# Scores of two heads on the two row halves of TensorE in all layers, and a re-ordered even layer, in a two-block transformer on one core

## The chip, the core and the metric

The kernel runs on one core of a Trainium2 chip. The metric is the device time of one execution in microseconds. Before the change it is 2098.92 us, the median of three runs (2097.51 to 2102.35). Three engines matter for this change: TensorE (PE), which does the matmuls and the transposes and whose clock has two levels, 1.2 and 2.4 GHz; VectorE (DVE); and GpSimd (POOL). ScalarE (ACT) does the exponentials, the casts and the copies out of PSUM, and the SP queue issues the loads. Each engine works through its own list of instructions in order and waits on semaphores for the others.

## The reference, cut to what matters

The input has 256 tokens of width 1024. A first block of two layers is followed by a second block of an even and an odd layer. Every layer of the first block has a hybrid mixer of three attentions, then an attention to a memory and a feed-forward (in layer 0 a SwiGLU, in layer 1 a mixture of eight experts). The even layer has a 16-head causal attention and, beside it, a state space model.

```python
# hybrid mixer, per layer: 4 heads of 64 (neighborhood), 8 query heads on 2 key heads of 64 (GQA), 4 heads of 96 (MLA)
ya = neighborhood_attention(a_q, a_k, a_v, na_rpb)
yb = blocked_attention(qb.reshape(b, s, GQA_KV_HEADS, GQA_GROUP, HEAD_DIM), kb, vb, HEAD_DIM ** -0.5)
yc = blocked_attention(q_full, k_full, vc, (MLA_NOPE + MLA_ROPE) ** -0.5)
merged = gates[0] * (ya @ w_proj_a) + gates[1] * (yb @ w_proj_b) + gates[2] * (yc @ w_proj_c)

# even layer: rotation of the first 16 of 64 columns of each head, causal attention, and the state scan
rot = jnp.concatenate([x1 * cos - x2 * sin, x2 * cos + x1 * sin], axis=-1)
scores = jnp.einsum('bhqd,bhqkd->bhqk', q_blk, k_g)
_, states = lax.associative_scan(combine, (a_seq, bu), axis=1)      # 32 groups of 64 complex states
y = gelu(real(states @ c) + d_skip * u); y = y * sigmoid(y @ glu_w + glu_b)
```

## The kernel before, in words

**Linear layers.** A weight arrives in f32 by DMA, ACT casts it to a high part (L201) and DVE or POOL subtracts that from it for a low part (L203, `..._l`). Each product is three matmuls (L219 to L221). In the even layer every low part is made on POOL, as 128x1024 subtractions. The names say the weight: `weu` (state input), `weq` (queries and keys), `wev` (values), `wega` and `wegs` (gates of the attention and of the state branch), `wglu` (the linear layer behind the state branch, which needs all of its outputs), `wg` and `wp` (gates and projections of the hybrid mixer).

**Attention in the hybrid mixer.** `attend` walks over pairs of heads. For each head `att_scores` (matmul at L412) makes a 256 x 256 score in one bank of PSUM, two matmuls of 64 rows (96 for MLA). DVE takes the row maximum, ACT the exponential, PE transposes (L446), and `att_pv` multiplies by the values. The 64-row operands lie on partitions 0 to 63 or 64 to 127: in a neighborhood pair one head on each half, in a GQA pair (heads 2b and 2b+1, which share a key head) both on the same.

**Even layer.** `even` runs about from 1668 to 1877 us of the trace. `state` makes the state input. `qk(i, c)` makes queries or keys of eight heads (i says which, c which half) and rotates them by six DVE products (L1400) before four transposes per half of the tokens (L1404). `attend(b)` handles two heads: scores (L1335, L1336), maximum (L1341 on DVE), exponential (L1345, ACT), reciprocal (L1346, DVE), scaling (L1348, ACT), transposes (L1356), a copy (L1357, ACT) and the product with the values (L1366, L1367). The state model is a generator `ssm` with 16 steps, here called pairs: two groups of states each. A pair has two matmuls into one bank (`bu`, L1273, 32 rows), then fifteen DVE instructions in that bank (L1282 to L1304: rotation, two scans in two halves, rotation back). After each four pairs come sixteen matmuls (`sy`, L1311), a DVE sum (L1314) and the GELU.

**PSUM.** There are three banks `ps`, two `sc`, one `pv` and two `tp` (the transposes'). In the even layer `bu` alternates between a `ps` and an `sc` bank, the scores are in `sc`, and the transposes in `tp`.

**What sets the order.** A scheduler in the framework takes the program's order of emission as the priority, and puts each engine's instructions in the order in which its own model says that they become ready. The program emits `state`, `qk(0,0)`, `qk(1,0)`, two pairs, `values(0)`, one pair, and then eight `attend(b)` with two pairs behind each but the first, with the remaining `qk`, `values` and `gate_s` between them.

Of the kernel before, what the change touches and what calls it, by code (L numbers as in the profile page):

```python
# [19 lines left out]
P = 128  # L20
T = 256
# [75 lines left out]
class Net:  # L97
# [305 lines left out]
        return xo  # L403


    def att_scores(self, q, k):

        ps = self.mmps("sc", "sc")
        n = len(q)
        for t in range(2):  # L410
            for j in range(n):
                self.nc.tensor.matmul(ps[:, ts(t, T)], q[j][:, ts(t, P)], k[j], start=(j == 0), stop=(j == n - 1))  # L412
        return ps

    def att_probs(self, ps, scale, bias=None, pr=None):
# [40 lines left out]
    def att_pv(self, vs, pTs):  # L456

        ps = self.mmps("pv", "pv")
        for i in range(2):
            o = ps[64 * i:64 * i + 64, :T]  # L460
            for kb in range(2):
                self.nc.tensor.matmul(o, vs[i][kb], pTs[i][:, kb], start=kb == 0, stop=kb == 1, skip_group_check=True)
        return ps[:, :T]

    def rope(self, dst, src, cos, sin, half, tmp):
# [22 lines left out]
    def hybrid(self, x, l):  # L488
# [73 lines left out]
        def attend(pairs, y0, scale, bias=None):  # L562

            def finish(b, hs, pTs):
                o = self.att_pv([vv for _, _, vv in hs], pTs)
                self.split(o, yT[0][:, y0 + b], yT[1][:, y0 + b])
            for b, hs in enumerate(pairs):
                pTs = []
                for i, (q, k, _) in enumerate(hs):
                    pr = None  # L570
                    if bias is not None:
                        pr = act.tile([P, 2, T], F32, tag="pr", name="nab", bufs=4)
                        nc.sync.dma_start(pr, bias[2 * b + i].rearrange("(t q) k -> q t k", q=P))
                    pTs.append(self.att_pT(self.att_probs(self.att_scores([q], [k]), scale, pr, pr)))
                finish(b, hs, pTs)

        def hv(f, h):
# [36 lines left out]
        ml = [[(qcT[:, 2 * b + i], kcT[:, 2 * b + i], [vc[t][:, 2 * b + i] for t in range(2)]) for i in range(2)]  # L614
              for b in range(2)]
        attend(ml, 6, 96 ** -0.5)
        attend([[gq(2 * b), gq(2 * b + 1)] for b in range(4)], 2, 0.125)


        gt, mg, mx = {}, [], []  # L620
# [638 lines left out]
    def ssm(self, u):  # L1259
# [6 lines left out]
        for po in range(4):  # L1266
            del zs[:]
            for pq in range(4):
                p = 4 * po + pq
                rows = slice(32 * pq, 32 * pq + 32)  # L1270
                ps = self.mmps("bu", ("ps", "sc")[p % 2])
                for j in range(2):
                    mm(ps[:, ts(j, T)], self.bmat[rows, po, j], u[rows, po], start=True, stop=True,  # L1273
                       tile_position=(32 * pq, 0))
                c = self.rot[:, 0, p, :HT].unsqueeze(1).to_broadcast(B)
                s = self.rot[:, 1, p, :HT].unsqueeze(1).to_broadcast(B)
                m1 = act.tile([P, 2, T], F32, tag="sm1", name="sm1", bufs=5)
                q = [act.tile([P, 2, T], F32, tag="sm2", name="sm2", bufs=4) for _ in range(2)]
                z = ps.rearrange("p (j t) -> p j t", t=T)
                zr = ps.rearrange("p (j t) -> p j t", t=HT)  # L1280
                qr = [a.rearrange("p j t -> p (j t)").rearrange("p (j t) -> p j t", t=HT) for a in q]
                v.tensor_tensor(qr[0], zr, s, op=ALU.mult)  # L1282
                v.tensor_tensor(zr, zr, c, op=ALU.mult)
                v.tensor_tensor(z[:, 0], z[:, 0], q[0][:, 1], op=ALU.add)
                v.tensor_tensor(z[:, 1], z[:, 1], q[0][:, 0], op=ALU.subtract)
                r = self.decay[:, p:p + 1].to_broadcast([P, HT])
                init = [0.0, 0.0]
                for h in range(NH):
                    if h:
                        ini = self.sm.tile([P, 2], F32, tag="sini", name="sini")  # L1290
                        e = h * HT - 1
                        v.tensor_scalar(ini, z[:, :, e], self.rot[:, 0, p, HT:HT + 1], None, op0=ALU.mult)
                        v.scalar_tensor_tensor(ini[:, 0:1], z[:, 1, e:e + 1], self.nsin[:, p:p + 1], ini[:, 0:1],
                                               op0=ALU.mult, op1=ALU.add)
                        v.scalar_tensor_tensor(ini[:, 1:2], z[:, 0, e:e + 1], self.rot[:, 1, p, HT:HT + 1],
                                               ini[:, 1:2], op0=ALU.mult, op1=ALU.add)
                        init = [ini[:, 0:1], ini[:, 1:2]]
                    for j in range(2):
                        o = z[:, j, ts(h, HT)]
                        v.tensor_tensor_scan(o, r, o, init[j], op0=ALU.mult, op1=ALU.add)  # L1300
                v.tensor_tensor(qr[1], zr, s, op=ALU.mult)
                v.tensor_tensor(zr, zr, c, op=ALU.mult)
                v.tensor_tensor(m1[:, 0], z[:, 0], q[1][:, 1], op=ALU.subtract)
                v.tensor_tensor(m1[:, 1], z[:, 1], q[1][:, 0], op=ALU.add)  # L1304
                zs.append(m1)
                if pq < 3:
                    yield
# [20 lines left out]
        self.nc.scalar.activation(s, u, AF.Tanh, scale=0.5)  # L1328
        self.nc.vector.scalar_tensor_tensor(dst, s, 1.0, u, op0=ALU.add, op1=ALU.mult)

    def causal_probs(self, pr, q, k, scale, bias):

        nc, v = self.nc, self.nc.vector
        ps = self.mmps("sc", "sc")
        nc.tensor.matmul(ps[:, :P], q[:, :P], k[:, :P], start=True, stop=True)  # L1335
        nc.tensor.matmul(ps[:, P:3 * P], q[:, P:], k, start=True, stop=True)  # L1336
        mx, ng, sm = (self.sm.tile([P, 2], F32, tag=n, name=n, bufs=4) for n in ("mx", "ng", "sm"))
        cols = [slice(0, P), slice(P, 3 * P)]
        parts = [pr[:, c] for c in cols]
# [20 lines left out]
    def causal_pv(self, vs, pTs):  # L1360

        ps = self.mmps("pv", "pv")
        mm = self.nc.tensor.matmul
        for i in range(2):
            o = ps[64 * i:64 * i + 64, :T]
            mm(o, vs[i][0], pTs[i][:, :T], start=True, stop=False, skip_group_check=True)  # L1366
            mm(o[:, P:], vs[i][1], pTs[i][:, T:], start=False, stop=True, skip_group_check=True)  # L1367
        return ps[:, :T]

    def even(self, x):  # L1370
# [18 lines left out]
        def qk(i, c):  # L1389
# [7 lines left out]
            lo, hi = h4[:, :, :, :8], h4[:, :, :, 8:16]  # L1397
            for o, p, q, op in ((t1, lo, si, ALU.mult), (t2, hi, si, ALU.mult), (lo, lo, co, ALU.mult),
                                (hi, hi, co, ALU.mult), (lo, lo, t2, ALU.subtract), (hi, hi, t1, ALU.add)):
                v.tensor_tensor(o, p, q, op=op)  # L1400
            for t in range(2):
                tp = self.tps()
                for b in range(4):
# [10 lines left out]
        def attend(b):  # L1414
            if b % 2:
                prs = [self.sm.tile([P, 512], F32, tag="lnf", name="epr", bufs=LNF) for i in range(2)]
            else:
                prs = [self.keep.tile([P, 512], F32, tag=n, name="epr") for n in ("lngt", "lnbt")]
            pTs = [self.causal_pT(self.causal_probs(prs[i][:, :3 * P], *(a[64 * i:64 * i + 64, b] for a in qkT),
                                                    0.125, bias)) for i in range(2)]  # L1420
            if b % 2 == 0:
                self.lin_feat(x, w, 3072 + P * b, 256, lambda i, ps: gate(b + i, ps), name="wega")
            o = self.causal_pv([[vv[:, t, 64 * (2 * b + i):64 * (2 * b + i) + 64] for t in range(2)]
# [6 lines left out]
        with self.phase("ssm"):  # L1430
# [11 lines left out]
                              name="wegs")  # L1442
            state()
            self.hold = None
            qk(0, 0)
            qk(1, 0)
            step(2)
            values(0)
            step(1)
            late = [lambda: qk(0, 1), lambda: qk(1, 1), lambda: values(1), lambda: gate_s(0), lambda: gate_s(1)]  # L1450
# [112 lines left out]
def layout(inputs):  # L1563
# [8 lines left out]
    order = np.arange(a["w_in"].shape[2])  # L1572
    order[768:1280] = 768 + np.arange(512).reshape(2, 4, 64).transpose(1, 0, 2).reshape(-1)
    I["w_in"] = a["w_in"][:, :, order]

    def cols(v):
        return v.reshape(-1, P).T
# [77 lines left out]
```

## Time and profile before

The profiled execution took 2097.21 us by the clock of the runs, and its trace has a span of 2095.4 us. The median of the three runs is 1.7 us above the profiled execution.

| what | value |
|---|---|
| runs, us | 2102.35, 2097.51, 2098.92 |
| profiled execution, us | 2097.21 |
| its span in the trace, us | 2095.4 |
| PE busy, share of the span | 96% |
| DVE busy | 79% |
| ACT busy | 62% |
| POOL busy | 13% |

PE is busy nearly everywhere, so a microsecond of PE work is in most places a microsecond of time. The exception is where PE's busy share falls. Rows of the timeline give the start of a group of like instructions, its length, the engine, the line, the operation with output and inputs, and the count; a bracket at the end holds the idle time before it and the instruction that ended it. The trace shows two instructions for each f32 matmul of the program, so a score of two matmuls has four rows in it.

### The profile page before, as it was taken

The page shows a single profiled execution, that of the slowest core. Times are in us where ns is not written, and L with a number is a line of the kernel's source. Part 1 is how long each engine was busy: PE and PEld are TensorE (multiplying, and loading weights), DVE is VectorE, ACT ScalarE, POOL GpSimd, SP SyncE. Part 2 cuts the span into 40 slices and gives each one's busy share as a digit, 9 for nine tenths or more (in the row PEclk, how much of TensorE's full clock was granted, in tenths as well). Part 3 has the DMA queues.
Part 4 walks back from the last instruction along what each step waited for, and adds up shares of the span by engine and source line. Part 5 has one row for each costly group of instructions (what it writes and reads, how often), then busy time and mean ns, then how long its engine had stood idle before and what let it go on. Part 6 is the DMA issues. An engine that isn't in the chain of part 4 may idle for free. (4 is left out here: it accounts for less than half of the span.)

```text
span 2095.4 us, 31534 instructions
## 1 busy us (share of the span) xinstructions
PE 2008.7 (96%) x11112; PEld 1706.1 (81%) x11112; DVE 1647.7 (79%) x2958; ACT 1302.9 (62%) x1968; POOL 280.4 (13%) x169
## 2 busy tenths in 40 slices
PE   8999998999999999899999999999999799968998
PEld 8877898998987888688888888888888587737996
DVE  7775765555786676799999999999999747987984
ACT  5665545444666454777887787778778545624452
POOL 2000223000400140200000000000000375402400
PEclk9999999999999999899999999999999799969999
DMA  8544545555644548699999899999999664305562
GB/s 284 165 137 148 188 147 166 185 182 188 209 142 131 191 154 288 225 338 359 345 343 350 290 366 312 367 317 372 311 394 327 209 178 122 108 27 158 182 197 95
DMA packets 300423, 481.84 MB, mean 230 GB/s; under 512 B 18528, under 2 KB 117856, under 8 KB 300256
## 3 DMA queue, kind: packets, MB, share of 16 engines
q1 hardware_dynamic: 300256, 479.75, 68.0%
q8 instruction: 89, 1.46, 0.3%
q14 instruction: 78, 0.64, 0.1%
HBM read 478.63 MB, written 1.05 MB: 229 GB/s over the span
## 5 line engine op out<-in xcount | busy, mean ns | idle before, releaser
L203 DVE TENSOR_TENSOR we_l<-we_r,we_h 128x1024 fp32r<-128x1024 f32 (+1 forms) x188 | 208.2, 1129 | 12.0 <-ACT we_h L201 8.9
L201 ACT CAST we_h<-we_r 128x1024 fp32r<-128x1024 f32 (+1 forms) x188 | 181.4, 978 | 53.9 <-PE eg L220 22.1
L221 PE MATMUL ea<-we_l,xgh 128*128 128x512 f32 (+1 forms) x384 | 146.6, 382 | 0.4 <-DVE we_l L203 0.4
L219 PE MATMUL ea<-we_h,xgh 128*128 128x512 f32 (+1 forms) x384 | 144.9, 377 | 0.9 <-ACT xgh L210 0.9
L219 PE MATMUL eg<-we_h,xgh 128*128 128x512 f32 (+1 forms) x384 | 145.6, 379 | 0.0
L221 PE MATMUL eg<-we_l,xgh 128*128 128x512 f32 (+1 forms) x384 | 144.8, 377 | 0.4 <-DVE we_l L203 0.2
L220 PE MATMUL ea<-we_h,xgl 128*128 128x512 f32 (+1 forms) x384 | 144.8, 377 | 0.3 <-DVE xgl L211 0.3
L220 PE MATMUL eg<-we_h,xgl 128*128 128x512 f32 (+1 forms) x384 | 143.7, 374 | 0.0
L203 DVE TENSOR_TENSOR we_l<-more,we_h 128x1024 fp32r<-128x1024 f32 (+1 forms) x120 | 133.5, 1132 | 12.7 <-ACT we_h L201 10.0
L221 PE MATMUL ey<-wd_l,ehh 128*128 128x512 f32 x352 | 138.2, 396 | 1.8 <-DVE wd_l L203 1.6
L201 ACT CAST we_h<-more 128x1024 fp32r<-128x1024 f32 (+1 forms) x120 | 116.0, 978 | 38.1 <-PE eg L220 13.3
L220 PE MATMUL ey<-wd_h,ehl 128*128 128x512 f32 x352 | 138.1, 392 | 0.0
L219 PE MATMUL ey<-wd_h,ehh 128*128 128x512 f32 x352 | 138.0, 392 | 0.0
L203 POOL TENSOR_TENSOR weu_l<-we_r,weu_h 128x1024 fp32r<-128x1024 f32 x4 | 9.4, 2372 | 793.1 <-ACT weu_h L201 793.1
L203 DVE TENSOR_TENSOR wd_l<-wd_r,wd_h 128x1024 fp32r<-128x1024 f32 x87 | 103.8, 1217 | 1.8 <-ACT wd_h L201 1.1
L219 PE MATMUL gu<-xh,wgu_h 128*128 128x256 f32 x352 | 100.9, 287 | 0.9 <-ACT xh L210 0.9
L201 ACT CAST wd_h<-wd_r 128x1024 fp32r<-128x1024 f32 x87 | 90.0, 1052 | 17.9 <-PE ey L220 16.5
L220 PE MATMUL gu<-xh,wgu_l 128*128 128x256 f32 x352 | 100.6, 286 | 0.0
L221 PE MATMUL gu<-xl,wgu_h 128*128 128x256 f32 x352 | 100.3, 286 | 0.0
L201 ACT CAST wres_h<-wres_r 128x1024 fp32r<-128x1024 f32 x54 | 56.6, 1052 | 68.1 <-PE ps L220 59.4
L203 DVE TENSOR_TENSOR wgu_l<-wgu_r,wgu_h 128x1024 fp32r<-128x1024 f32 x44 | 55.4, 1259 | 51.0 <-ACT wgu_h L201 51.0
L203 DVE TENSOR_TENSOR wres_l<-wres_r,wres_h 128x1024 fp32r<-128x1024 f32 x46 | 56.1, 1224 | 43.1 <-ACT wres_h L201 42.6
(631 smaller groups left out, 6513.5 us busy)
## 6 DMA issues: line engine op xcount, KB each, us to landing
we_r<-in_moe_w_gu_dram SPq DMA_DIRECT2D x156, 512.0 KB, 5.4
more<-in_moe_w_gu_dram SPq DMA_DIRECT2D x100, 512.0 KB, 5.6
wd_r<-in_moe_w_down_dram SPq DMA_DIRECT2D x87, 512.0 KB, 7.4
more<-in_moe_w_down_dram SPq DMA_DIRECT2D x60, 512.0 KB, 7.2
rt<-in_moe_w_gu_dram SPq DMA_DIRECT2D x49, 512.0 KB, 5.5
wg_r<-in_w_in_dram SPq DMA_DIRECT2D x48, 512.0 KB, 3.7
wgu_r<-in_ffn_w_gu_dram SPq DMA_DIRECT2D x44, 512.0 KB, 4.5
rt<-in_moe_w_down_dram SPq DMA_DIRECT2D x29, 512.0 KB, 7.5
```

Source lines behind the costliest of these rows:

```text
L201: nc.scalar.copy(H[:, a:b], r)
L203: sub.tensor_tensor(L[:, a:b], r, H[:, a:b].bitcast(F32), op=ALU.subtract)
L219: mm(ps, sH, mH, start=first, stop=False, skip_group_check=skip)
L220: mm(ps, sL, mH, start=False, stop=False, skip_group_check=skip)
L221: mm(ps, sH, mL, start=False, stop=last, skip_group_check=skip)
```

## The change

There are two parts, and the number of matmuls stays as it was.

**Hybrid mixer.** `att_scores` now takes a list of heads and walks over the two halves of the queries in the outer loop, over the heads in the inner one, with one `sc` bank for each head. Pairs of 64-row heads go in together; MLA heads go in one by one, as before. The GQA pairs are now heads b and b+4, which lie on different row halves, and the rows of `w_proj_b` are permuted on the host to match. In `att_pv` the loop over the key blocks is the outer one.

**Even layer.** All `bu` banks are `sc` banks. The scores of both heads are made together by `causal_scores`, in the `tp` banks. The six products of each rotation are issued on GpSimd, 24 in all. `causal_pv` interleaves its two heads. The order of emission has two pairs ahead of `qk(0,0)` and one each behind `qk(0,0)`, `qk(1,0)` and `values(0)`: five pairs instead of three ahead of the first `attend`.

```diff
-    def att_scores(self, q, k):
-        ps = self.mmps("sc", "sc")
-        n = len(q)
-        for t in range(2):
-            for j in range(n):
-                self.nc.tensor.matmul(ps[:, ts(t, T)], q[j][:, ts(t, P)], k[j], start=(j == 0), stop=(j == n - 1))
+    def att_scores(self, heads):
+        ps = [self.mmps("sc", "sc") for _ in heads]
+        for t in range(2):
+            for o, (q, k) in zip(ps, heads):
+                self.nc.tensor.matmul(o[:, ts(t, T)], q[:, ts(t, P)], k, start=True, stop=True)
...
+                split = all(q.shape[0] == 64 for q, _, _ in hs)
+                if split:
+                    sc = self.att_scores([(q, k) for q, k, _ in hs])
...
-        attend([[gq(2 * b), gq(2 * b + 1)] for b in range(4)], 2, 0.125)
+        attend([[gq(b), gq(b + 4)] for b in range(4)], 2, 0.125)
...
-                ps = self.mmps("bu", ("ps", "sc")[p % 2])
+                ps = self.mmps("bu", "sc")
...
+    def causal_scores(self, heads):
+        ps = [self.tps("sc") for _ in heads]
+        for cols, keys, qs in ((slice(0, P), slice(0, P), slice(0, P)), (slice(P, 3 * P), slice(0, T), slice(P, T))):
+            for o, (q, k) in zip(ps, heads):
+                self.nc.tensor.matmul(o[:, cols], q[:, qs], k[:, keys], start=True, stop=True)
+        return ps
...
-                v.tensor_tensor(o, p, q, op=op)
+                nc.gpsimd.tensor_tensor(o, p, q, op=op)
...
+            step(2)
             qk(0, 0)
+            step(1)
             qk(1, 0)
-            step(2)
+            step(1)
             values(0)
             step(1)
```

On PE, at the start of the even layer's queries, the first two pairs stand here before: `bu` is the output of a pair's matmuls, `su` the state input and `ssb` the state matrix.

```order
11747 L219 MATMUL ps<-weq_h,xh 128x512
11748 L220 MATMUL ps<-weq_h,xl 128x512
11749 L1273 MATMUL bu<-su,ssb 128x256
11750 L221 MATMUL ps<-weq_l,xh 128x512
11751 L219 MATMUL ps<-weq_h,xh 128x512
```

And on PE in the changed kernel, where the first two pairs stand right behind the last `weu` matmul and the first two `weq` matmuls:

```order
11658 L221 MATMUL ps<-xl,weu_h 128x256
11659 L219 MATMUL ps<-weq_h,xh 128x512
11660 L220 MATMUL ps<-weq_h,xl 128x512
11661 L1276 MATMUL bu<-su,ssb 128x256 x4
11662 L221 MATMUL ps<-weq_l,xh 128x512
```

Two pairs moved from the middle of the `weq` matmuls, one pair's first matmul at a time, to their very start.

On PE, at the end of the even layer, the rows ahead of the first `wglu` matmul before: `tp` are the transposes of the probabilities, `pv` the product with the values, `sy` the outputs of four pairs.

```order
12387 L1273 MATMUL bu<-su,ssb 128x256 x2
12388 L1356 MATMUL tp<-ident,epr 128x128 x3
12389 L1366 MATMUL pv<-pT,ev 64x256
12390 L1367 MATMUL pv<-pT,ev 64x128
12391 L1356 MATMUL tp<-ident,epr 128x128 x3
12392 L1366 MATMUL pv<-pT,ev 64x256
12393 L1367 MATMUL pv<-pT,ev 64x128
12394 L1311 MATMUL sy<-sm_26501,ssck 32x256
```

And on PE in the changed kernel, the last pair and what follows it:

```order
12337 L1276 MATMUL bu<-su,ssb 128x256 x2
12338 L1374 MATMUL pv<-pT,ev 64x256
12339 L1364 MATMUL tp<-ident,epr 128x128
12340 L1339 MATMUL sc<-ekT,eqT 128x128
12341 L1339 MATMUL sc<-ekT,eqT 128x256
12342 L1364 MATMUL tp<-ident,epr 128x128 x2
12343 L1374 MATMUL pv<-pT,ev 64x256
12344 L1376 MATMUL pv<-pT,ev 64x128 x2
12345 L1339 MATMUL sc<-ekT,eqT 128x128
12346 L1339 MATMUL sc<-ekT,eqT 128x256
12347 L1314 MATMUL sy<-sm_26381,ssck 32x256
```

The last pair now stands ahead of the last two heads' scores, and the scores of two heads (`sc`) stand apart, with transposes of the earlier head between them; so it is for the head pairs 3 to 7, while 0 to 2 stand together.

On POOL, between the low parts of the queries' and the values' weights, this stands in the changed kernel (before, the second row is followed at once by the sixth):

```order
71 L203 TENSOR_TENSOR weq_l<-we_r,weq_h 128x1024 x2
72 L203 TENSOR_TENSOR weq_l<-weq_r,weq_h 128x1024 x6
73 L1409 TENSOR_TENSOR etmp<-rt,rope_e 128x128 x2
74 L1409 TENSOR_TENSOR rt<-rt,rope_e 128x16x8 x2
75 L1409 TENSOR_TENSOR rt<-rt,etmp 128x16x8 x2
76 L203 TENSOR_TENSOR wev_l<-wev_r,wev_h 128x1024 x4
```

The six products of a rotation came onto POOL's queue as a block between the weights' low parts.

## Rows read from the trace of the kernel before

**Rows 1.** Windows: stretch, length, busy us per engine (instructions), PE clock, DMA share, GB/s.
```profile
100.00:200.00 100.00, 100.00 (x492) 77.95 (x492) 67.71 (x133) 56.59 (x107) 0.00 (x0) 1.00 0.45 138
600.00:700.00 100.00, 100.00 (x496) 77.92 (x496) 70.83 (x150) 57.41 (x115) 0.00 (x0) 1.00 0.46 135
1830.00:1840.00 10.00, 5.05 (x32) 3.36 (x34) 9.67 (x22) 2.70 (x5) 0.00 (x0) 0.76 0.52 158
1840.00:1872.00 32.00, 17.18 (x60) 7.69 (x60) 28.87 (x82) 7.14 (x22) 0.00 (x0) 0.50 0.00 1
```
**Rows 2.** Waits of PE, 1668 to 1880 us: line, waited for, total, times, longest.
```profile
PE sy L1311 <- DVE sm L1303: 14.8, 3, 5.4
PE bu L1273 <- DVE mx L1341: 3.3, 1, 3.3
```
**Rows 3.** Timeline of PE: scores of the hybrid mixer, line L412.
```profile
62.84 1.14 PE L412 MATMUL sc<-naqk 64*128 64x256 f32 x8
65.63 1.13 PE L412 MATMUL sc<-naqk 64*128 64x256 f32 x4
67.23 0.70 PE L412 MATMUL sc<-naqk 64*128 64x256 f32 x2
68.23 0.70 PE L412 MATMUL sc<-naqk 64*128 64x256 f32 x2
136.04 1.99 PE L412 MATMUL sc<-kb,qb 64*128 64x256 f32 x8
665.75 1.99 PE L412 MATMUL sc<-kb,qb 64*128 64x256 f32 x8
```
**Rows 4.** Timeline of DVE in the even layer: a rotation, and pairs.
```profile
1696.04 2.19 DVE L1400 TENSOR_TENSOR etmp<-rt,rope_e 128x128 f32<-128x128 f32 x2 [11.63 <-ACT rt L1387]
1709.07 0.69 DVE L1282 TENSOR_TENSOR sm<-bu,rot 128x512 f32<-128x512 f32 x1 [10.04 <-PE bu L1273]
1723.49 0.68 DVE L1282 TENSOR_TENSOR sm<-bu,rot 128x512 f32<-128x512 f32 x1
1746.91 0.69 DVE L1282 TENSOR_TENSOR sm<-bu,rot 128x512 f32<-128x512 f32 x1 [1.63 <-PE bu L1273]
1863.04 0.68 DVE L1282 TENSOR_TENSOR sm<-bu,rot 128x512 f32<-128x512 f32 x1
1870.11 0.41 DVE L1304 TENSOR_TENSOR sm<-bu,sm 128x256 f32<-128x256 f32 x1
```
**Rows 5.** Windows as in rows 1: the even layer in two stretches.
```profile
1731.00:1745.00 14.00, 14.00 (x65) 9.81 (x64) 6.43 (x26) 10.92 (x28) 7.14 (x4) 1.00 0.31 92
1745.00:1872.00 127.00, 106.50 (x618) 76.89 (x616) 116.54 (x329) 59.01 (x140) 40.35 (x17) 0.85 0.30 94
```
**Rows 6.** Line L1400, 1740 to 1790 us: operation, count, ns min/median/max, first and last start.
```profile
L1400 DVE TENSOR_TENSOR etmp<-rt,rope_e x4: 279/595/1891, 1748.1 to 1764.8; 128x128 f32<-128x128 f32 x4
L1400 DVE TENSOR_TENSOR rt<-rt,rope_e x4: 277/279/280, 1750.7 to 1766.5; 128x128 f32<-128x128 f32 x4
L1400 DVE TENSOR_TENSOR rt<-rt,etmp x4: 273/276/282, 1751.8 to 1767.2; 128x128 f32<-128x128 f32 x4
```
**Rows 7.** Timeline of POOL in the even layer.
```profile
1695.50 2.38 POOL L203 TENSOR_TENSOR weq_l<-weq_r,weq_h 128x1024 fp32r<-128x1024 f32 x1 [0.32 <-ACT weq_h L201]
1701.72 9.62 POOL L203 TENSOR_TENSOR wev_l<-wev_r,wev_h 128x1024 fp32r<-128x1024 f32 x4 [3.85 <-ACT wev_h L201]
```
**Rows 8.** Timeline of PE: a score of head pair 3, a head's scores, the end.
```profile
1796.51 0.49 PE L1335 MATMUL sc<-ekT,eqT 64*128 64x128 f32 x2
...
1841.78 0.79 PE L1335 MATMUL sc<-ekT,eqT 64*128 64x128 f32 x2
1842.37 1.06 PE L1336 MATMUL sc<-ekT,eqT 64*128 64x256 f32 x2
...
1872.09 0.58 PE L219 MATMUL ps<-sgxh,wglu_h 128*128 128x256 f32 x1
```
**Rows 9.** Timeline of ACT: the copy that ends that head's chain.
```profile
1852.72 0.48 ACT L1357 COPY pT<-tp 128x384 f32<-128x384 f32 x1 [0.50 <-PE tp L1356]
```

More of the change, by code (lines that the diff above doesn't have):

```diff
@@ L458, in att_pv @@
         ps = self.mmps("pv", "pv")
[L459 to L462, printed above, removed]
+        for kb in range(2):
+            for i in range(2):
+                self.nc.tensor.matmul(ps[64 * i:64 * i + 64, :T], vs[i][kb], pTs[i][:, kb], start=kb == 0,
+                                      stop=kb == 1, skip_group_check=True)
         return ps[:, :T]
@@ L573, in attend @@
                         nc.sync.dma_start(pr, bias[2 * b + i].rearrange("(t q) k -> q t k", q=P))
-                    pTs.append(self.att_pT(self.att_probs(self.att_scores([q], [k]), scale, pr, pr)))
+                    pTs.append(self.att_pT(self.att_probs(s, scale, pr, pr)))
                 finish(b, hs, pTs)
@@ L1329, in silu2, with causal_probs @@
         self.nc.vector.scalar_tensor_tensor(dst, s, 1.0, u, op0=ALU.add, op1=ALU.mult)
-    def causal_probs(self, pr, q, k, scale, bias):
+    def causal_scores(self, heads):
[4 more added lines that the diff above has]
+        return ps
+    def causal_probs(self, pr, ps, scale, bias):
         nc, v = self.nc, self.nc.vector
-        ps = self.mmps("sc", "sc")
-        nc.tensor.matmul(ps[:, :P], q[:, :P], k[:, :P], start=True, stop=True)
-        nc.tensor.matmul(ps[:, P:3 * P], q[:, P:], k, start=True, stop=True)
         mx, ng, sm = (self.sm.tile([P, 2], F32, tag=n, name=n, bufs=4) for n in ("mx", "ng", "sm"))
@@ L1363, in causal_pv @@
         mm = self.nc.tensor.matmul
+        o = [ps[64 * i:64 * i + 64, :T] for i in range(2)]
         for i in range(2):
-            o = ps[64 * i:64 * i + 64, :T]
-            mm(o, vs[i][0], pTs[i][:, :T], start=True, stop=False, skip_group_check=True)
-            mm(o[:, P:], vs[i][1], pTs[i][:, T:], start=False, stop=True, skip_group_check=True)
+            mm(o[i], vs[i][0], pTs[i][:, :T], start=True, stop=False, skip_group_check=True)
+        for i in range(2):
+            mm(o[i][:, P:], vs[i][1], pTs[i][:, T:], start=False, stop=True, skip_group_check=True)
         return ps[:, :T]
@@ L1418, in attend @@
                 prs = [self.keep.tile([P, 512], F32, tag=n, name="epr") for n in ("lngt", "lnbt")]
-            pTs = [self.causal_pT(self.causal_probs(prs[i][:, :3 * P], *(a[64 * i:64 * i + 64, b] for a in qkT),
-                                                    0.125, bias)) for i in range(2)]
+            sc = self.causal_scores([[a[64 * i:64 * i + 64, b] for a in qkT] for i in range(2)])
+            pTs = [self.causal_pT(self.causal_probs(prs[i][:, :3 * P], sc[i], 0.125, bias)) for i in range(2)]
             if b % 2 == 0:
@@ L1574, in layout @@
     I["w_in"] = a["w_in"][:, :, order]
+    I["w_proj_b"] = a["w_proj_b"][:, order[768:1280] - 768]
     def cols(v):
```

1 line of the change is left out of this document (added).

## Prediction

> **What bounds the kernel now.** I first read the windows, because the share of busy time over the whole span hides the stages. In the two stretches of the hybrid mixer that hold its GQA scores, PE is busy for all of the 100 us, at the full clock, while DVE has a third of its time left [rows 1]. There the kernel is bound by PE, and a microsecond taken from PE is a microsecond of time. In the even layer this turns over. From 1830 us PE is busy for 5.05 of 10 us, then for 17.18 of 32 us at a granted clock of 0.50, the level of 1.2 GHz, and DVE is busy for 38.5 of the 42 us [rows 1]. There the end is set by DVE. The view of waits says what is late: PE's `sy` matmuls wait 14.8 us in all for the last DVE instructions of a pair, and one `bu` waits 3.3 us for a score bank that DVE empties [rows 2]. What counts as the end of the even layer is the first `wglu` matmul, at 1872.09 [rows 8], since it needs all of the pairs. So I cost the hybrid part by PE time and the even part by DVE's work ahead of that matmul.
>
> **Scores in the hybrid mixer.** Two heads on different row halves, four matmuls, lasted 1.14 us (a neighborhood pair at 62.84). Two on the same half, with as many columns, lasted 1.99 (GQA, the first at 136.04, the last of eight at 665.75) [rows 3]. So the row halves work at the same time, and the GQA pairs should go from 1.99 to 1.14: 8 x 0.85 = 6.8 us. The second neighborhood pair of a layer was torn into three pieces, 1.13 + 0.70 + 0.70 = 2.53 us [rows 3]; its four matmuls now come together, 1.39 us less. The rows of the timeline overlap by nearly 0.1 us with what follows each piece, so I take 1.2, and twice for the two layers: 2.4 us. The MLA scores stay. Sum: 9.2 us, all of it on the path, since PE has no gap there [rows 1]. The low end is below nothing: a pair now takes both `sc` banks at once, so the next pair's scores wait for DVE's maxima of both heads. DVE has 32 us of every 100 free [rows 1], which speaks against such a wait, but if each of the 12 pairs of row-half heads in both layers lost 0.8 us, the gain would be gone, and at 1.5 us it would be a loss of 9. I take 9.2, since PE has other matmuls to do between the pairs. The interleaving in `att_pv` changes no count and its heads were already side by side: nothing.
>
> **Pairs moved forward in the even layer.** DVE waited 11.63 us for the first rotation and 10.04 us for the first pair, which began at 1709.07; the third began at 1723.49, and the fourth only at 1746.91, when its matmul had come; between 1731 and 1745 DVE was busy for 6.43 of 14 us [rows 4, 5]. The changed order on PE has two pairs at the start of `weq` and three more before the first `attend`, then two again where the fourth and the fifth stood. So at 1745 DVE will have five pairs behind it rather than three, and the two moved ones went into time in which it was idle. A pair costs DVE 7.48 us from the start of the last L1282 to the end of its L1304 [rows 4], less two instructions of 0.33 us of the pair before that lie in between: 6.8. Two pairs are 13.6 us.
>
> **Rotations on GpSimd.** Of the four rotations the last two lie behind 1745. Their twelve products took 279 ns each at the least, but the first of each lasted up to 1891 ns [rows 6], some 5 us together. The first rotation shows why: its first product started at 1696.04 and, with the next, took 2.19 us, while POOL's subtraction ran from 1695.50 to 1697.88 [rows 4, 7]. The two earlier rotations lie where DVE was idle and bring nothing. The Trainium skill, SBUF — State Buffer, "SBUF: two separate sides", says that VectorE and GpSimd share one pair of ports under an exclusive lock, so that a VectorE instruction with two SBUF inputs and a GpSimd instruction never run at once; the trace agrees, by the 2.19 us just named. By that rule the moved products still stop DVE's instructions of that kind. The twelve products would then give 12 x 0.30 = 3.6 of the 5 us back, as an estimate by that page's lock, and the forecast would be 3.6 us later.
>
> On POOL the price has no row. The bounds are DVE's 0.28 us for the same product [rows 6] and POOL's 2.38 us for eight times the columns [rows 7]; by columns 2.38 / 8 = 0.30, and I take that, since L203 is the same operation with two inputs. Six products are 1.8 us. They stand in POOL's queue ahead of the low parts of `wev`, which would wait behind them; POOL had 3.85 us idle there, waiting for ACT [rows 7], so they fit. That cover is gone from 0.64 us per product on. At 2.38 us a block of six would hold POOL for 14.3 us and PE would wait 10 us for `wev`; I keep this end for the range.
>
> **Banks.** `bu` in `sc` banks alone removes the tie of a `bu` bank to a weight's `ps` bank and to the scores' maxima; 3.3 us of PE's waits were of that kind [rows 2], inside the stretch that DVE sets, so they are worth nothing by themselves. Three head pairs have their scores together on the two row halves. One head's scores took 1.65 us at the half clock (1841.78 to 1842.37 + 1.06) [rows 8], 0.83 at the full one, so PE gets 3 x 0.83 = 2.5 us back, but PE doesn't set the end. The `tp` banks are where a new wait can come from (rival 3).
>
> **The sum.** From 1745 to 1872 DVE was busy for 116.5 us and idle for 10.5 [rows 5]. Without two pairs and two rotations 97.9 us are left. With the same idle time the `wglu` matmul starts at 1745 + 97.9 + 10.5 = 1853.4. DVE is now less far behind PE and will wait for it more often, between 0 and 6 us more; I take 2.6, so 1856, 16 us earlier. The end that PE alone would set is 1830 + 5.05 + 17.18 / 2 = 1843.6 at the full clock [rows 1], less 2.5 for the scores: 1841. DVE stays later than that, so 1856 stands. What follows `wglu` moves along as a whole. 2097.2 - 9.2 - 16 = 2072.0 for an execution like the profiled one; the median of the runs is 1.7 above it, so 2073.7.
>
> **Rivals.**
> 1. *PE becomes the bound.* If DVE keeps up, `wglu` starts at 1841, 31 us earlier: 2097.2 - 9.2 - 31 + 1.7 = 2058.7. For it: DVE's remaining 97.9 us fit into the 96 us from 1745 to 1841 almost exactly. Against it: that needs a DVE that never waits, and it waited 10.5 us before.
> 2. *The even layer gains nothing.* If the maxima, exponentials and transposes of the last heads form the path rather than DVE's sum of work, the end stays at 1872 and only the hybrid part is left: 2097.2 - 9.2 + 1.7 = 2089.7. For it: in the changed order scores, transposes and value products of the last heads alternate on PE up to the end.
> 3. *The `tp` banks make the heads go one after the other; slower.* In the head pairs 3 to 7 a head's scores now take one of the two banks through which the transposes go, and the second head's scores stand behind the first one's transposes. One head's chain, from its score at 1841.78 to the end of its copy at 1853.20, is 11.4 us [rows 8, 9]. Head pair 3 began at 1796.51 [rows 8]. Ten chains with nothing overlapped end at 1796.5 + 114 = 1910.5, 38.4 us later than before, and the time is 2097.2 - 9.2 + 38.4 + 1.7 = 2128. It is slower than before by more than the measurement tells from ten chains of 8.9 us on (1872.1 + 9.2 + 4.2 = 1885.5). Against it: much of the 11.4 us is DVE at other pairs' work, which is lighter now, and one head needs its bank only until its maximum is taken.
> 4. *The row halves bring nothing* (the change doesn't do what it says): the even part alone, 2097.2 - 16 + 1.7 = 2082.9. Against it stands 1.14 next to 1.99 us [rows 3].
>
> **How the numbers follow.** The forecast, with the even part between 10 and 22 us, gets 0.52. Rival 1 gets 0.13, rival 2 gets 0.17, rival 3 gets 0.07, rival 4 gets 0.04. For a loss in the even layer that cancels the hybrid gain (between rivals 2 and 3) I leave 0.07. A measurement of this kernel tells some 0.2%, 4.2 us, from no change. Faster is then 0.52 + 0.13 + 0.17 + 0.04 = 0.86, the same 0.07, slower 0.07. The range goes up to 2090, which takes in rival 2, and down to 2062, which leaves out half of rival 1 and so holds about 0.8.
>
> **What would show it.** The GQA scores should be groups of eight rows of 1.14 us. DVE's first L1282 (now L1285) should start near 1686, five of them should lie ahead of the first maximum's end, and the first `wglu` should come some 25 us earlier in the span, of which some 9 are there when the even layer starts. POOL's products should last about 0.3 us. PE should still wait for DVE ahead of the last `sy`, at half clock, but for less time. The prediction is wrong if PE waits in the hybrid mixer for maxima, if DVE shows idle time of more than 17 us between 1745 and the end, or if PE waits for weights' low parts behind POOL's products.

## The result, and the profile after

The changed kernel takes 2075.63 us, the median of four runs (2073.2 to 2080.89), against 2098.64 for the kernel before in the same comparison (2097.51 to 2102.35). The ratio is 0.9891, with a 95% interval of 0.9867 to 0.9914. The forecast was 2073.7 us, within 2062 to 2090. The span in the trace went from 2095.4 to 2072.5 us.

Where the 23 us went can be read off PE's timeline, since the order of the matmuls is nearly the same in both kernels. I compare the start of the same matmul in both, at the borders of the stages:

| border | before | after | gained so far |
|---|---|---|---|
| first `wc` (hybrid mixer, layer 0) | 40.91 | 40.41 | 0.50 |
| first `wres` behind it | 211.11 | 206.12 | 4.99 |
| first `wc`, layer 1 | 548.35 | 543.42 | 4.93 |
| first `wres` behind it | 719.42 | 710.32 | 9.10 |
| first expert matmul | 851.10 | 840.50 | 10.60 |
| first `weq` (even layer) | 1683.44 | 1672.45 | 10.99 |
| first `wglu` | 1872.09 | 1849.09 | 23.00 |
| end of the span | 2095.4 | 2072.5 | 22.9 |

The two hybrid mixers give 4.49 and 4.17 us, 8.7 together. The memory attention of layer 1 gives another 1.5 us; its code is the same, and the granted clock between 700 and 800 us was 0.98 before and 1.00 after. The even layer, from the first `weq` to the first `wglu`, went from 188.65 to 176.64 us: 12.0. I call these 176.64 us "the stretch" from here on.

The scores of the hybrid mixer, timeline of PE after (start, length, engine, line, operation, output and input, rows and columns, form, count):

```profile
62.34 1.13 PE L411 MATMUL sc<-naqk 64*128 64x256 f32 x8
65.65 1.55 PE L411 MATMUL sc<-naqk 64*128 64x256 f32 x8
134.34 1.13 PE L411 MATMUL sc<-kb,qb 64*128 64x256 f32 x8
...
657.91 1.14 PE L411 MATMUL sc<-kb,qb 64*128 64x256 f32 x8
```

The GQA pairs went from 1.99 [rows 3] to 1.13 or 1.14 us, all eight. The second neighborhood pair came together, but took 1.55 us; the run with the loops swapped shows why.

The even layer, windows of the kernel after (stretch, length, busy us and instructions of PE, PE's loads, DVE, ACT and POOL, then PE's clock, the DMA share and GB/s):

```profile
1720.00:1734.00 14.00, 14.00 (x70) 10.84 (x69) 4.43 (x12) 11.40 (x24) 11.57 (x6) 1.00 0.49 143
1734.00:1849.00 115.00, 103.48 (x592) 75.68 (x590) 99.13 (x294) 60.29 (x148) 42.93 (x28) 0.87 0.30 98
1802.00:1814.00 12.00, 8.72 (x30) 6.30 (x31) 11.38 (x35) 5.73 (x18) 2.36 (x1) 0.57 0.13 45
```

The first two answer to [rows 5], shifted by the 11 us gained ahead of them. DVE's work in the second fell from 116.5 to 99.1 us, and its idle time rose from 10.5 to 15.9. The third shows a stretch at a granted clock of 0.57, most of it at the level of 1.2 GHz, in the middle of the layer; the kernel before does not have it there.

The timeline of DVE after, with its idle times in brackets:

```profile
1674.17 0.69 DVE L1285 TENSOR_TENSOR sm<-bu,rot 128x512 f32<-128x512 f32 x1 [0.77 <-PE bu L1276]
...
1698.94 0.69 DVE L1285 TENSOR_TENSOR sm<-bu,rot 128x512 f32<-128x512 f32 x1 [4.34 <-PE bu L1276]
1712.57 0.48 DVE L1317 SCALAR_TENSOR_TENSOR su<-su,pp,sy 128x256 f32<-128x256 f32 x1 [6.67 <-PE sy L1314]
1714.01 0.69 DVE L1285 TENSOR_TENSOR sm<-bu,rot 128x512 f32<-128x512 f32 x1 [0.96 <-PE bu L1276]
1734.20 0.42 DVE L1435 TENSOR_TENSOR sil<-pv,ega 128x256 f32<-128x256 f32 x1 [7.54 <-PE pv L1376]
1735.25 0.69 DVE L1285 TENSOR_TENSOR sm<-bu,rot 128x512 f32<-128x512 f32 x1 [0.63 <-PE bu L1276]
```

The first pair starts at 1674.17 instead of 1709.07 [rows 4], the fifth at 1714.01, and the sixth at 1735.25. DVE still waits 6.67 and 7.54 us between them.

What PE waits for in the even layer after, 1657 to 1860 us (line, waited for, total, times, longest):

```profile
PE tp L1364 <- ACT epr L1356: 9.4, 4, 4.5
PE pv L1374 <- ACT pT L1365: 2.1, 3, 1.0
```

The wait of `sy` for DVE, 14.8 us before [rows 2], is gone from this view. PE now waits 9.4 us with its transposes for scaled probabilities, and the wait of `bu` for score maxima is gone as well.

### The profile page after: what moved, and what is told of

Read it like the earlier page. It is cut to its first block, busy times and chain, and to the rows that moved or that the text cites. A ratio compares the mean times of both kernels' runs of the same rounds, so it can differ in the third digit from the quotient of the medians.

```text
span 2072.5 us, 31525 instructions
## 1 busy us (share of the span) xinstructions
PE 1992.7 (96%) x11112; PEld 1694.1 (82%) x11112; DVE 1634.5 (79%) x2934; ACT 1301.8 (63%) x1968; POOL 290.9 (14%) x193
```

## The experiments

Each kernel below is given with its time, and with the first `weq` and the stretch in the trace of one of its executions. The times of one kernel differ by 0.6 to 7.7 us from execution to execution. The places in a trace are exact to some hundredths, but they hold for that one execution. The kernel before took 2100.89, 2099.33 and 2097.56 us (medians) beside the three groups of runs.

| kernel | time, us | first `weq` | stretch | span |
|---|---|---|---|---|
| before | 2098.64 | 1683.44 | 188.65 | 2095.4 |
| after | 2075.63 | 1672.45 | 176.64 | 2072.5 |
| hybrid mixer alone | 2089.09 | 1672.01 | 191.74 | 2086.8 |
| even layer alone | 2085.05 | 1683.62 | 175.08 | 2083.2 |
| pairs' order of before | 2083.32 | 1672.28 | 185.22 | 2081.0 |
| banks of before | 2072.59 | 1673.48 | 176.08 | 2072.8 |
| rotations on DVE | 2074.94 | 1672.60 | 176.41 | 2073.1 |
| no rotations | 2074.03 | 1671.95 | 175.94 | 2072.1 |
| GQA on the same row half | 2081.59 | 1680.33 | 175.08 | 2079.8 |
| heads one after the other | 2081.46 | 1677.48 | 181.31 | 2081.7 |
| after, once more | 2074.16 | 1672.82 | 176.64 | 2072.9 |
| two more pairs ahead | 2071.02 | 1672.66 | 165.21 | 2069.3 |
| one more pair ahead | 2069.29 | 1672.19 | 169.13 | 2067.3 |
| two more pairs, banks of before | 2067.59 | 1673.87 | 167.46 | 2066.3 |

### Each half of the change alone

The edit is the diff's own: the hybrid part put into the kernel before, and the even part put into the kernel before.

> The kernel before with the change of the hybrid mixer alone (scores of two heads on the row halves, GQA pairs b and b+4); the even layer as before. Theory (row halves work at the same time, PE sets the end there): the first weq matmul of the even layer starts 9 to 11 us earlier than the 1683.44 of before, as in the changed kernel (1672.45), and the stretch from the first weq to the first wglu matmul stays at 188.7 +- 1 us; the time is 2088 +- 2. Rival (the two parts act only together, by freeing banks or the queue): less than 5 us earlier at weq, or a stretch that is shorter than 186.

Measured: 2089.09 us (2088.32 to 2090.19), the ratio to the kernel before 0.9945 (0.9928 to 0.9961). The first `weq` came 11.4 us earlier, a little more than expected. The stretch was not the same: 191.74, 3.1 us longer with the same code as before. PE's rows are equal to 0.02 us for the first 127 us of it, and then part:

```profile
1799.00:1807.00 8.00, 8.00 (x34) 5.73 (x33) 6.53 (x25) 4.00 (x14) 0.28 (x1) 0.57 0.19 66
```

This is a window of the hybrid part alone. PE was busy for all of its 8 us, but at a granted clock of 0.57. In the kernel before the same matmuls, 11 us later, ran at 1.00:

```profile
1810.00:1818.00 8.00, 8.00 (x57) 6.71 (x57) 7.93 (x29) 5.75 (x17) 0.70 (x1) 1.00 0.20 68
```

So the hybrid part is worth 11.4 us up to the even layer, of which the mixers have 9.0 in this trace, and 3 us were lost again to the clock in code that the part does not touch.

> The kernel before with the change of the even layer alone; the hybrid mixer as before. Theory (DVE's work ahead of wglu sets the end of the even layer, whatever came before it): the first weq within 1 us of 1683.4, the stretch from the first weq to the first wglu 176.6 +- 1 us as in the changed kernel (188.7 before), and the time 2087 +- 2. Rival (part of the 12 us comes from loads that were further ahead): a stretch over 179.

Measured: 2085.05 us (2084.98 to 2085.55), ratio 0.9925 (0.9908 to 0.9942). The first `weq` is where it was before, and the stretch is 175.08, 13.6 us shorter than before and 1.6 shorter than in the changed kernel. That is half a microsecond outside the expected 176.6 +- 1. The even part stands by itself; what came ahead of it gives it nothing. The 1.6 us are again the clock: here the fall in the middle of the layer was short.

### Which piece of the even layer pays

The pairs' order of before, in the changed kernel:

```diff
             self.hold = None
-            step(2)
             qk(0, 0)
-            step(1)
             qk(1, 0)
-            step(1)
+            step(2)
             values(0)
             step(1)
```

> The changed kernel with the order of emission of before in the even layer (three pairs ahead of the first attend rather than five); banks and rotations stay changed. Theory (the two pairs moved into DVE's idle time are the larger term, 13.6 us less what idle time comes back): the stretch from the first weq to the first wglu grows from 176.6 to 183 to 188 us, and the time to 2083 to 2087. Rival (the banks are what counts: a bu bank no longer waits for scores or weights): the stretch stays below 180.

Measured: 2083.32 us (2081.91 to 2084.02), the stretch 185.22. Taking the two pairs back costs 8.6 us of the 12.0, and 7.7 to 9.2 us by the times (against 2075.63 and 2074.16). The theory holds, and the rival, banks, falls. PE's waits show the old pattern again, in this kernel from 1655 us on:

```profile
PE sy L1314 <- DVE sm L1306: 8.1, 2, 4.5
PE tp L1364 <- ACT epr L1356: 3.9, 3, 2.2
```

The banks of before, in the changed kernel:

```diff
-                ps = self.mmps("bu", "sc")
+                ps = self.mmps("bu", ("ps", "sc")[p % 2])
...
-        ps = [self.tps("sc") for _ in heads]
+        ps = [self.mmps("sc", "sc") for _ in heads]
```

> The changed kernel with the banks of before in the even layer: bu alternates between a ps and an sc bank, and the scores (of both heads together) are in sc banks; order of emission and rotations stay changed. Theory (banks move no DVE work): the stretch from the first weq to the first wglu stays within 3 us of 176.6, and the time within 3 us of 2075.6. Rival (the banks are what counts): the stretch goes back to 184 or more, and PE's waits of bu for mx show again.

Measured: 2072.59 us (2071.74 to 2074.58), the stretch 176.08. With these banks the first pairs' matmuls stand ahead of the first `weq`, which so starts 1.0 us later; the span, 2072.8, says the same. The time is 3.0 us under the 2075.63 of the changed kernel and 1.6 under its 2074.16 when run again, so the banks are worth little or nothing in this order. PE waits for other things between 1734 and 1850 us, and ends at the same time:

```profile
PE sy L1314 <- DVE sm L1306: 5.8, 2, 3.6
PE sc L1339 <- DVE mx L1349: 4.2, 2, 2.8
PE tp L1364 <- ACT epr L1356: 1.2, 1, 1.2
```

Of the 9.4 us that PE waited with transposes, 1.2 are left, and 10 us of waits for DVE have come in their place.

The rotations, back on DVE and left out:

```diff
-                nc.gpsimd.tensor_tensor(o, p, q, op=op)
+                v.tensor_tensor(o, p, q, op=op)
```

> The changed kernel with the 24 rotation products back on DVE. Theory (twelve of them lie where DVE has work, 5 us): the stretch from the first weq to the first wglu grows from 176.6 to 180 to 183 us. Rival 1 (the shared lock: on GpSimd they stop DVE nearly as long): the stretch grows by less than 2 us. Rival 2 (the pairs ahead leave DVE idle there anyway, or PE's rotation transposes come earlier without GpSimd's longer products): no growth, or a shorter stretch.

Measured: 2074.94 us (2074.8 to 2075.94), the stretch 176.41, 0.2 us shorter than with GpSimd. The theory falls: the 5 us of my sum are not there. DVE's window over the same 115 us of this kernel shows why; DVE is the third busy time, and the changed kernel had 99.13 there:

```profile
1734.00:1849.00 115.00, 104.47 (x591) 76.74 (x591) 100.92 (x306) 61.15 (x148) 38.08 (x16) 0.86 0.31 97
```

Its twelve products take 3.90 us in their own rows, not 5; DVE's busy time as a whole grows by 1.8 us, since other rows are shorter, and the 1.8 us came out of idle time.

> The changed kernel without the 24 rotation products, on any engine (queries and keys stay unrotated; everything else is as in the changed kernel). It measures what the products still cost on GpSimd. Theory (they are hidden on GpSimd): the stretch from the first weq to the first wglu is within 1 us of 176.6. Rival (shared lock, or weights' low parts held up behind them in GpSimd's queue): 2 to 5 us shorter.

Measured: 2074.03 us (2073.15 to 2075.99), the stretch 175.94, 0.7 us shorter than with the products. On GpSimd they are hidden, as the theory says. They last 0.47 us each, in the changed kernel (count, ns min/median/max, first and last start):

```profile
L1409 POOL TENSOR_TENSOR etmp<-rt,rope_e x8: 453/467/477, 1688.1 to 1751.0; 128x128 f32<-128x128 f32 x8
L1409 POOL TENSOR_TENSOR rt<-rt,rope_e x8: 458/468/649, 1688.9 to 1751.8; 128x128 f32<-128x128 f32 x8
```

### The row halves

GQA pairs as before, all else changed:

```diff
-        attend([[gq(b), gq(b + 4)] for b in range(4)], 2, 0.125)
+        attend([[gq(2 * b), gq(2 * b + 1)] for b in range(4)], 2, 0.125)
...
-    I["w_proj_b"] = a["w_proj_b"][:, order[768:1280] - 768]
```

> The changed kernel with the GQA pairs of before (heads 2b and 2b+1, both on the same row half), the scores of two heads still issued together in turn. Theory (the row halves are the gain): groups of eight rows take 1.9 to 2.0 us again rather than 1.14, and the first weq starts 6 to 7 us later than 1672.45. Rival (issuing both heads together is the gain): groups shorter than 1.9 us, weq less than 4 us later.

Measured in a single run: 2081.59 us, the first `weq` 7.9 us later, a little more than expected. The mixers took 3.3 and 4.1 us more than in the changed kernel (first `wc` to first `wres`: 169.0 and 171.0 against 165.7 and 166.9), 7.4 us together; outside the mixers 2.5 us were lost and 2.0 gained. The groups are long again:

```profile
135.02 1.99 PE L411 MATMUL sc<-kb,qb 64*128 64x256 f32 x8
```

So it is the halves, not the issuing together.

The loops of `att_scores` swapped, so that a head's two matmuls follow each other:

```diff
-        for t in range(2):
-            for o, (q, k) in zip(ps, heads):
+        for o, (q, k) in zip(ps, heads):
+            for t in range(2):
```

> The changed kernel with the loops of att_scores swapped: both matmuls of one head, then both of the other, on the two row halves. In the changed kernel the second neighborhood pair came in this order by the scheduler and took 1.55 us instead of 1.14; in the kernel before, the first neighborhood pair had this order and took 1.14. Theory A (taking the heads in turn matters): groups of 1.55 us, and the first weq 3 to 4.5 us later than 1672.45. Theory B (the order doesn't matter where PE's queue is ahead): groups of 1.14 us, weq within 1.5 us.

Measured: 2081.46 us (2079.03 to 2083.47). All GQA groups took 1.14 us, as theory B says:

```profile
136.37 1.14 PE L411 MATMUL sc<-kb,qb 64*128 64x256 f32 x8
65.97 1.13 PE L411 MATMUL sc<-naqk 64*128 64x256 f32 x4
67.58 0.70 PE L411 MATMUL sc<-naqk 64*128 64x256 f32 x2
68.57 0.70 PE L411 MATMUL sc<-naqk 64*128 64x256 f32 x2
```

But the second neighborhood pair of each layer was torn into three again. The first `weq` came 5.0 us later: 1.2 and 1.1 us in the two mixers, 0.8 ahead of the first mixer, 1.5 in layer 1's memory attention, as in the kernel before, and the rest in small pieces. I had expected weq within 1.5 us for theory B, and missed that by the torn pairs and by what had nothing to do with the loops.

Why a group takes 1.55 us in the changed kernel is a wait and not the order. In the second neighborhood pair the second head's first row starts at 66.07 us, 0.42 us behind the first head's. It needs the score bank of the pair before, and DVE ends the last maximum of that pair at 66.01 us. The timeline shows the wait at the weight loads (PEld) of these matmuls:

```profile
65.65 0.93 PEld L411 LDWEIGHTS sc<-naqk 64*128 64x128 f32 x7 [0.30 <-DVE mx L425]
65.93 0.08 DVE L425 DVE_READ_ACCUMULATOR2_ANT mx<- 128x1 f32 x1
```

1.14 and 0.42 make the 1.55. The same wait stands at the same place in layer 1, and in the runs of the hybrid part alone and of the GQA pairs on one half. So theory A falls for these groups too.

### The same code, different times

Four executions of kernels with the same even layer had stretches of 175.08, 175.08, 176.64 and 181.31 us. Up to 128.7 us all PE rows agree to 0.02 us. Then comes a fall of the clock to its lower level, 1.2 GHz, of different length. Windows around it, of the even layer alone, of the changed kernel and of heads one after the other:

```profile
1815.00:1822.00 7.00, 4.54 (x21) 3.77 (x22) 6.91 (x23) 2.81 (x9) 1.08 (x1) 0.76 0.23 75
```

```profile
1802.00:1814.00 12.00, 8.72 (x30) 6.30 (x31) 11.38 (x35) 5.73 (x18) 2.36 (x1) 0.57 0.13 45
```

```profile
1807.00:1829.00 22.00, 18.54 (x69) 14.35 (x70) 16.70 (x48) 8.49 (x25) 2.35 (x1) 0.53 0.11 30
```

I took the length for chance, and ran the changed kernel again.

> The changed kernel itself, once more. The stretch from the first weq to the first wglu matmul came out between 175.1 and 181.3 us in three kernels with the same even layer (changed kernel, even part alone, heads one after the other), and all of the difference began behind 129 us of the stretch, where the granted clock was at 0.50 for 4 to 20 us. Theory (the length of the stretch at half clock is chance, not the code): every instruction up to 128 us of the stretch within 0.1 us of the changed kernel's first profile, and behind it a stretch at half clock whose length alone gives the difference. Rival (the code ahead of the even layer sets it): the stretch is 176.6 +- 0.2 again, with the same 12 us at half clock.

Measured: 2074.16 us (2073.14 to 2075.23), and a stretch of 176.64 to the hundredth, with the same fall:

```profile
1802.00:1814.00 12.00, 8.68 (x31) 6.22 (x31) 11.70 (x36) 6.11 (x18) 2.35 (x1) 0.57 0.14 45
```

The two traced executions agree, as the rival says, but they do not decide it. The mean granted clock and the span of every execution are on record. The four of the changed kernel's first comparison have spans of 2071.2, 2072.5, 2075.0 and 2079.1 us at clocks of 0.978, 0.977, 0.974 and 0.973, and heads one after the other had 2077.2 to 2081.7 us at 0.976 to 0.974; its traced execution, with the longest fall, was the slowest. So the clock of one kernel does differ between executions, where in the kernel is not on record, and whether the code ahead or chance sets the length of this fall stays open. A stretch read from a single trace can carry such a difference.

In the changed kernel the clock is at its upper level up to 1803 us and falls there, in windows and in the timeline of PE:

```profile
1802.00:1803.00 1.00, 0.10 (x1) 0.10 (x2) 1.00 (x5) 1.00 (x3) 0.45 (x1) 1.00 0.06 16
1803.00:1804.00 1.00, 0.92 (x2) 0.09 (x2) 0.93 (x3) 1.00 (x6) 1.00 (x1) 0.52 0.00 0
```

```profile
1802.90 1.01 PE L1374 MATMUL pv<-pT,ev 128*64 128x256 f32 x2 [0.99 <-ACT pT L1365]
1806.29 0.48 PE L1364 MATMUL tp<-ident,epr 128*128 128x128 f32 x1 [2.37 <-ACT epr L1356]
1806.69 1.65 PE L1339 MATMUL sc<-ekT,eqT 64*128 64x128 f32 x4
```

The fall comes behind a wait of 0.99 us for a copy of probabilities, and ahead of the wait of 2.37 us. The scores at 1806.69 take 1.65 us, the length at half clock [rows 8]. But the hybrid part alone had a fall of the same kind with PE busy throughout, as the profile counts it, in the 19 us ahead of it too, so a gap is not needed for it.

### More pairs ahead

DVE's 7.54 us of idle time ahead of 1734.20 say that more pairs could go there. One or two pairs behind the first `attend`:

```diff
-                if b:
-                    step(2)
+                step(2)
```

> The changed kernel with two pairs behind the first attend as well (seven ahead of the second attend rather than five). Theory (pairs moved into DVE's idle time are the one term that pays; DVE was idle for 7.5 us from 1726 on, waiting for the first value products): the stretch from the first weq to the first wglu is 4 to 8 us shorter than 176.6, and the time 2067 to 2072. Rival (the chain of the last heads sets the end now): less than 2 us shorter, or longer, since the last heads have no pairs beside them.

Measured: 2071.02 us (2070.46 to 2071.6). The time is within the expected range, the stretch is not: 165.21, 11.4 us shorter. DVE's idle time from 1720 to 1734 is gone, 12.89 us busy instead of 4.43:

```profile
1720.00:1734.00 14.00, 14.00 (x66) 10.49 (x66) 12.89 (x33) 9.19 (x21) 9.07 (x4) 1.00 0.45 132
```

But the span fell by 3.2 us only. The pairs are finished earlier, so `wglu` starts earlier, and the last heads' value products fall behind it: the last of them starts 183.5 us after the first `weq`, against 181.3 in the changed kernel.

```profile
1856.14 0.38 PE L1376 MATMUL pv<-pT,ev 128*64 128x128 f32 x2
```

PE is busy for 24.70 of the 26 us from 1838 to 1864 us: what the last heads need of it now stands behind the first `wglu` instead of ahead of it. So the larger part of the 11.4 us is lost again to the last heads, as the rival said; its number, less than 2 us on the stretch, was wrong.

> The changed kernel with one pair behind the first attend (six ahead of the second attend rather than five). Theory: one pair moved, half of the gain of two: the stretch is 2 to 6 us shorter than 176.6. Rival (the chain of the last heads sets the end): within 1.5 us of it.

Here the line is `step(2 if b else 1)`. Measured: 2069.29 us (2066.95 to 2070.04), the stretch 169.13, 7.5 us shorter, more than expected, and the span 5.2 us shorter than the changed kernel's. One pair ahead is better than two, by 1.7 us, with ranges that don't touch.

> The changed kernel with two pairs behind the first attend as well, and with the banks of before (bu alternating, both heads' scores in sc). Theory (banks are worth nothing, pairs ahead are): within 2 us of the run with the two pairs alone. Rival (with more pairs ahead, bu in sc alone or the scores in the transposes' banks become the limit): 3 us or more shorter than that run.

Measured: 2067.59 us (2066.25 to 2068.3), ratio to the kernel before 0.9851 (0.9834 to 0.9867), the lowest median of all, though its range overlaps that of one more pair. The stretch is 2.3 us longer than with the two pairs alone, close to the theory, but the span is 3.0 us shorter. The time, 3.4 us shorter with ranges that don't touch, speaks for the rival: with more pairs ahead the banks count. Which of the two changes of banks counts, no run shows.

```profile
PE tp L292 <- DVE h L1094: 3.7, 2, 2.1
PE ps L219 <- DVE sm L1307: 3.1, 1, 3.1
PE sy L1314 <- DVE sm L1306: 2.7, 2, 1.6
```

These are its largest waits of PE between 1657 and 1890 us; the wait of transposes for probabilities is 0.9 us in all. It beats the changed kernel by 6.6 us in the same comparison (2074.16 for the changed kernel run again), with ranges that don't touch.

## Why the prediction was right, point by point

**What bounds it.** PE in the hybrid mixer held: the score groups lost 8.8 us by their rows, and the mixers 8.7 at their borders. DVE in the even layer held for the pairs: their order, which changes no engine's work, is worth 8.6 us. It did not hold for the last 9 us ahead of the first `wglu`. There DVE is busy for 6.24 us only, and the chain that ended last runs, but for 1.6 us of DVE rows, over scores, exponentials and transposes of the last heads, at the lower clock. That is the path of rival 2, in the window and in the critical chain after (start, length, what):

```profile
1840.00:1849.00 9.00, 6.50 (x26) 2.54 (x26) 6.24 (x22) 5.25 (x17) 0.00 (x0) 0.50 0.02 8
```

```profile
1840.00 1.59 PE sc L1339 x4
1843.36 0.49 ACT epr L1353 x2
1844.20 1.10 PE tp L1364 x3
1846.16 1.08 PE tp L1364 x3
1847.25 1.91 PE sy L1314 x10
```

The sign that PE would still wait for DVE ahead of the last `sy` did not come.

**Hybrid scores, 9.2 us forecast, 8.7 measured.** GQA 8 x 0.85 was right to the hundredth per group. The second neighborhood pair took 1.55 us rather than 1.14, twice. The wait for DVE's maxima, which the prediction held for its low end and named as a sign of being wrong, did come there: 0.42 us for one head, while PE worked on the other. The GQA pairs show no such wait, so the loss stayed at 0.8 us in all. The 1.5 us of the memory attention of layer 1 were not in the sum, and are the clock's.

**Pairs moved forward, 13.6 us forecast.** They are the term that pays, but taking them back costs 8.6. Where my step failed is the idle time: I held DVE's 10.5 us fixed and added 2.6, and it became 15.9. Of these, 10.6 us lie between 1734 and 1800 us, in small waits for what PE and ACT deliver, while PE is busy without a gap at the full clock:

```profile
1734.00:1800.00 66.00, 66.00 (x422) 53.37 (x421) 55.37 (x155) 36.24 (x78) 40.58 (x27) 1.00 0.43 138
```

With its pairs done earlier DVE catches up with PE there, and 2.8 us more are the last 9 us shown above.

**Rotations, 5 us forecast, 0 measured.** This term was wrong, and it is the one that the sum could have done without. I priced the products by their length in the trace. The first ones of the two blocks lasted 1.89 and 0.91 us, against 0.28 for the others [rows 6], while a POOL subtraction ran (from 1747.47 to 1749.85 us beside the first), and I counted all of it as work on the path. Back on DVE the products add 1.8 us to its busy time and no time at the end. GpSimd's price was too low as well, 0.47 us against 0.30 by columns. The block of six, 1.8 us in the sum, became 2.6, which still fitted. The loss that the Trainium skill's lock would bring (SBUF — State Buffer, "SBUF: two separate sides"), 3.6 us by my estimate, does not show at the end of the stretch: without any rotation it is 0.7 us shorter.

**Banks, 0 forecast, next to nothing measured** in the order of the change (176.08 against 176.64). With two more pairs ahead they cost 3 us of span, which I did not foresee.

**The sum.** The even layer gave 12.0 rather than 16: DVE's work was 99.1 us rather than 97.9, and its idle time 15.9 rather than 13.1, together 4.0 us. Of the single removals only the pairs' order costs anything, 8.6 us of the 12.0. Where the other 3.4 come from is not shown: it may be several pieces together, or the clock, which alone moves the stretch by 1.6 to 6.2 us in kernels with the same even layer, or the scores and value products of two heads made together in the even layer, which no run takes back. The 22.9 us of the whole are right because the hybrid part came to 11.0 at the first `weq`, 1.8 more than its sum, and the even part to 4 less. That these two misses have opposite signs is luck: 1.5 of the 1.8 us are the clock's. That what follows `wglu` moves along as a whole held for the change (23.00 us there, 22.9 at the end), but not with more pairs ahead.

**Rivals.** PE did not become the bound: PE-only would have had `wglu` at 1830 in the new time (1841 less 11), and it started at 1849.09; but from 1734 to 1800 us PE has no gap, so there its condition was met. Rival 2's path is there in the last 9 us, without its loss. The `tp` banks did make a new wait (rival 3), 9.4 us of PE's time, but not a loss: with the scores back in `sc` the end is the same.

## What to carry to other kernels

Where an engine sets the end of a stage, look for the time in which it was idle earlier in the same stage, and move independent work there; the order of emission alone was worth 8.6 us here, and one more pair another 5. Price work that is moved off that engine by what the engine does in its place, not by the length of the rows, since rows that lie beside another engine's instruction hold its time too. Make the landmark of a stage the last thing that the next one needs, or follow the span: a landmark that is only one of several inputs can move by 11 us while the span moves by 3.

## What the runs showed of the hardware that I had not expected

- The clock of PE fell to its lower level for most of 8 us with PE busy all of the time (1799 to 1807 us of the hybrid part alone, 0.57), in code that ran at 1.00 in the kernel before. PE had been busy in the 19 us ahead of it as well, last with matmuls of 32 and 64 rows and transposes.
- Two traced executions of the changed kernel have the same stretch to 0.01 us, while kernels with the same even layer and other code ahead of it differ by up to 6.2 us, all of it behind one fall. Other executions of one kernel differ by up to 7.9 us of span at mean clocks of 0.973 to 0.978, so two equal traces are no proof that a kernel keeps its falls.
- Two heads on different row halves took 1.13 or 1.14 us whether they were emitted in turn (the eight GQA groups of the changed kernel) or head by head (the ten whole groups of the run with the loops swapped). The 1.55 us of two groups are 0.42 us of waiting for a score bank.
- A product of 128 columns takes 0.47 us on GpSimd, a subtraction of 1024 columns 2.38: some 0.2 us are there whatever the columns, as an estimate from these two lengths alone (0.47 less 128 / 896 of the 1.91 between them).
